# Layer 0's shift and scale by slices of 128 columns from TensorE, and the first projections accumulated slice by slice in six banks

## The chip, the cores and the metric

The kernel runs on one core of one Trainium2 chip, in float32. The metric is the device time of one execution in microseconds (us), the median over executions. TensorE is called PE, VectorE DVE, ScalarE ACT, GpSimd POOL, and the queue that issues the transfers SP. PEld is PE's weight load, which the profile lists beside its matmuls.

## The reference, cut to what matters

Two trunk layers work on 1152 tokens: 128 context tokens (tile 0) and 1024 latent tokens (tiles 1 to 8), each with 1024 channels. Every layer begins in this way:

```python
mod = (jax.nn.silu(cvec) @ w_mod + b_mod).reshape(-1, 1, 3 * D_MODEL)
shift, scale, gate = jnp.split(mod, 3, axis=-1)
h = rms_norm(x, g_pre) * (1.0 + scale) + shift
fx, fz, rq, rk, rv, rz, aq, ak, av, az, mg = split_columns(h @ w_in)
```

Context tokens use one conditioning vector (`c_ctx`), latent tokens another (`c`), so the shift and the scale are two columns of 1024 numbers each: products of two vectors with a 1024x1024 part of `w_mod` (4 MB each). From `h` come all projections of the layer; then follow Fourier mixing, retention, windowed attention, the gates and the output projection.

## The kernel before

The framework orders the instructions of each engine ahead of time by a simulated schedule in which earlier program text has the higher priority. On the chip each engine works its list in order and waits on semaphores.

**Split operands.** `h` is kept transposed (channels on partitions, tokens along the free axis) in eight slices `k` of 128 channels, as a rounded part `HH` and a remainder `HL`. A weight unit is loaded into `raw` (512 KB), rounded to `hi` by ACT and its remainder `lo` is made by POOL (`split_unit`, L174 and L175). `unit_n2` loads 256 rows by 512 columns, so one unit serves two slices `k`; four units serve one group of 512 output columns. `proj_n` (L228 to L230) multiplies a token tile by a group: for each of eight slices three matmuls of 128x128 weights by 512 columns, HH by hi, HH by lo and HL by hi, all summed in one PSUM bank.

**Banks.** PSUM has eight banks: `pj` and `sl` two each, `sc` and `pv` one each, `tr` two.

**Startup, layer 0.** `startup` does the work ahead of the first projections. `prep` of a tile takes the row norm (ACT square, DVE and POOL for the root, DVE multiply), transposes eight blocks on PE and copies them to `xT`. Three tiles are prepared. Then the scale is made: each 128x1024 row block of `w_mod` (512 KB in rows of 4 KB) is multiplied on DVE by the two conditioning columns and summed into `dacc` (L335, L337), PE transposes the sums, and DVE reduces them to `sm`. The shift is made on PE: the conditioning columns are the weights (128x2) and 512 columns of `w_mod` stream past (L360), giving two rows, which are copied (L366), transposed (L369) and added to the bias (`sh`, L370). Then HH and HL of the three tiles are written (L377, L378), and the generator `g1` of the first group (`nat_group` with columns C_RK) can run: its four weight units, then tile by tile a projection into `pj`, rotary embedding on DVE, and a store. Tiles 3 to 5 and 6 to 8 are loaded, prepared and finished (`finish`, L387 to L390) while PE projects the tiles before them.

**After the first group** come the Fourier columns (L218 to L220, 384 tokens at a time), and so on to the end of the second layer.

Of the kernel before, what the change touches and what calls it, by code (L numbers as in the profile page):

```python
# [31 lines left out]
GK = 3  # L32
# [50 lines left out]
def hybrid_step(ctx, tc, ins, cst, outs):  # L83
# [199 lines left out]
    def startup(first):  # L283
        with pool("st", side="right") as st:
            def load_x(t):
                xt = mk(st, [P, D], "x0", bufs=3)
# [3 lines left out]
            xts = [load_x(t) for t in range(3)]  # L290
            cT = mk(st, [P, KT, 2], "cT")
            SP.dma_start(cT[:, :, 0], ins["c_ctx"].rearrange("(k p) -> p k", p=P))
            SP.dma_start(cT[:, :, 1], ins["c"][0].rearrange("(k p) -> p k", p=P))
            th = mk(st, [P, KT, 2], "cth")
# [3 lines left out]
            def chunk(tag, bufs):  # L298
                return mk(st, [P, KT, CH], tag, bufs=bufs)

            def prep(t, xt, xT):

                xh = norm_x(st, xt)
                for half in range(2):
                    pt = tr([P, 4, P])
                    for kk in range(4):
                        k = half * 4 + kk
                        PE.transpose(pt[:, kk, :], xh[:, k * P : (k + 1) * P], ident)
                    ACT.copy(xT[:, half * 4 : half * 4 + 4, t % 3 * P : (t % 3 + 1) * P], pt)

            xT = chunk("xT", 1)
            for t in range(3):
                prep(t, xts[t], xT)
            macc = [pj([2, 512]) for _ in range(2)]
            dacc = [mk(st, [P, D], f"dacc{s}") for s in range(2)]
            bm = mk(st, [P, 2, KT], "bm")
            gpr = mk(st, [P, KT], "gpr")
            wms = {}

            def stage(n):  # L320
                k, c0 = n % KT, 0 if n >= KT else D
                if n % 3 == 0:
                    wms["big"] = chunk("big", 2).rearrange("p a b -> p (a b)")
                wm = wms["big"][:, n % 3 * D : n % 3 * D + D]
                last_w[0] = SP.dma_start(wm, w_mod[0, k * P : (k + 1) * P, c0 : c0 + D]).ins
                return wm

            for k in range(KT):
                wm = stage(k)
                if k == 2:  # L330
                    SP.dma_start(bm, b_mod[0, 0 : 2 * D].rearrange("(s k p) -> p s k", p=P, k=KT))
                    SP.dma_start(gpr, g_pre[0].rearrange("(k p) -> p k", p=P))
                for s in range(2):
                    if k == 0:
                        DVE.tensor_scalar(dacc[s], wm, siluc[:, k, s : s + 1], None, op0=ALU.mult)  # L335
                    else:
                        DVE.scalar_tensor_tensor(  # L337
                            out=dacc[s], in0=wm, scalar=siluc[:, k, s : s + 1], in1=dacc[s], op0=ALU.mult, op1=ALU.add
                        )
            pr = mk(st, [P, KT, 2], "dred")  # L340
            for c in range(0, KT, 2):
                pt = (sc if c % 4 else sl)([P, 2, 2, P])
                for cc in range(2):
                    for s in range(2):
                        PE.transpose(pt[:, cc, s, :], dacc[s][:, (c + cc) * P : (c + cc + 1) * P], ident)
                DVE.tensor_reduce(pr[:, c : c + 2, :], pt, axis=AX.X, op=ALU.add)
            DVE.tensor_tensor(out=sm, in0=pr, in1=bm[:, 1, :].unsqueeze(2).to_broadcast([P, KT, 2]), op=ALU.add)
# [926 lines left out]
```

## Time and profile before

| what | us |
|---|---|
| median of 3 runs | 2020.54 (2018.04 to 2021.05) |
| the profiled execution, its own time | 2026.52 |
| its span, first to last instruction | 2024.7 |
| PE busy in the span | 1968.2 |
| DVE, ACT, POOL busy | 1033.1, 676.1, 551.5 |

The profiled execution is 6 us above the median of the runs, and 1.8 us of its time lie outside the span. Busy shares are averages over stages with different limits, and matmuls overlap in the records, so that the length of one is more than the step from one to the next.

### The profile page before, as it was taken

What the parts mean: (1) busy time and instruction counts of PE and PEld (TensorE: products, weight loads), DVE (VectorE), ACT (ScalarE), POOL (GpSimd) and SP (SyncE); (2) the same over time, 40 slices, a digit from 0 to 9 for tenths busy, and PEclk for the clock granted to TensorE, in tenths of its full rate; (3) what the DMA queues carried; (4) which work ended last, traced back from release to release, by engine and by line L of the source; (5) the groups of instructions that cost most, each with busy time, mean ns of one, the idle gap of its engine ahead of it and who ended that gap; (6) DMA issues with size and microseconds to landing.
All of it is one profiled execution on the core that took longest, in us unless ns stands there. A gap on an engine that the chain in (4) does not pass through costs nothing.

```text
span 2024.7 us, 30761 instructions
## 1 busy us (share of the span) xinstructions
PE 1968.2 (97%) x11334; PEld 1818.2 (90%) x11334; DVE 1033.1 (51%) x2675; ACT 676.1 (33%) x1563; POOL 551.5 (27%) x424
## 2 busy tenths in 40 slices
PE   5999999999999999999999999999999999999998
PEld 2898888999999999999877978799999999999987
DVE  6726556545677775414674262434356655531411
ACT  3522111214444555414331212022345554531411
POOL 2222232121122221254441203122121223234342
PEclk8999999999999999999999999999999999999999
DMA  8323553434343332333344134233333333342142
GB/s 293 100 71 100 155 148 117 129 117 137 112 123 114 114 102 65 116 118 128 118 142 96 58 94 146 82 118 95 124 107 102 108 101 97 93 132 90 55 146 93
DMA packets 245190, 230.58 MB, mean 114 GB/s; under 512 B 37920, under 2 KB 215856, under 8 KB 244784
## 3 DMA queue, kind: packets, MB, share of 16 engines
q1 hardware_dynamic: 245040, 228.62, 37.5%
q8 instruction: 89, 1.46, 0.3%
q14 instruction: 61, 0.50, 0.1%
HBM read 170.14 MB, written 58.42 MB: 113 GB/s over the span
## 4 chain that ended last, share of the span: by engine, by line
PE 88%; DVE 4%; DMA 4%; issue 1%; ACT 1%; SPq 1%; POOL 0%; DVEq 0%; POOLq 0%; ACTq 0%
PE pj L218 13%; PE pj L219 13%; PE pj L220 13%; PE pj L229 5%; PE pj L228 5%; PE pj L230 5%; PE pv L1099 4%; PE tr L1092 3%; PE sl L1038 2%; PE sl L941 2%; PE sl L943 2%; PE sl L942 2%; DMA raw<-in_w_in 2%; PE pj L941 2%; PE pj L942 2%; PE sl L230 2%
## 5 line engine op out<-in xcount | busy, mean ns | idle before, releaser
L218 PE MATMUL pj<-HH,uh 128*128 128x384 f32 x1440 | 496.0, 344 | 11.9 <-DVE XL L653 5.7
L220 PE MATMUL pj<-HH,ul 128*128 128x384 f32 x1440 | 491.5, 341 | 0.0
L219 PE MATMUL pj<-HL,uh 128*128 128x384 f32 x1440 | 489.6, 340 | 0.0
L175 POOL TENSOR_TENSOR ul<-raw,uh 128x1024 fp32r<-128x1024 f32 x80 | 193.6, 2421 | 513.9 <-ACT uh L174 420.4
L218 PEld LDWEIGHTS pj<-HH,uh 128*128 128x128 f32 x1440 | 273.5, 190 | 16.7 <-DVE XL L653 6.0
L219 PEld LDWEIGHTS pj<-HL,uh 128*128 128x128 f32 x1440 | 273.7, 190 | 0.7
L220 PEld LDWEIGHTS pj<-HH,ul 128*128 128x128 f32 x1440 | 273.3, 190 | 1.0
L174 ACT CAST uh<-raw 128x1024 fp32r<-128x1024 f32 x80 | 83.9, 1049 | 176.3 <-PE pj L219 108.2
L446 DVE SCALAR_TENSOR_TENSOR macc<-mw,siluc,macc 128x256 f32<-128x256 f32 x224 | 134.1, 639 | 8.4 <-DMA mw<-in_w_mod 8.4
L228 PE MATMUL pj<-uh,HH 128*128 128x512 f32 x336 | 134.1, 400 | 3.5 <-ACT kv L546 1.9
L229 PE MATMUL pj<-ul,HH 128*128 128x512 f32 x336 | 133.5, 397 | 0.0
L230 PE MATMUL pj<-uh,HL 128*128 128x512 f32 x336 | 132.9, 396 | 0.0
L1075 ACT ACTIVATE E<-E,NM 128x640 f32<-128x640 f32 (+1 forms) x128 | 101.8, 798 | 53.0 <-DVE NM L1071 52.9
L1095 ACT CAST Eh<-tr 128x512 fp32r<-128x512 f32 (+1 forms) x136 | 76.3, 574 | 113.9 <-PE tr L1092 101.0
L1096 DVE TENSOR_TENSOR El<-tr,Eh 128x512 fp32r<-128x512 f32 (+1 forms) x136 | 90.6, 671 | 36.3 <-ACT Eh L1095 29.7
L956 POOL TENSOR_TENSOR mth<-mth,ml 128x384 f32<-128x384 f32 x48 | 52.1, 1086 | 187.6 <-DVE mth L944 144.3
L944 DVE SCALAR_TENSOR_TENSOR M<-M,sl 128x384 f32<-128x384 f32 x48 | 26.5, 553 | 133.1 <-PE sl L943 132.6
L1056 DVE CUSTOM_DVE_ANT_0 E<-sl,mask,m 128x384 f32<-128x384 f32 (+1 forms) x128 | 71.9, 580 | 30.4 <-PE sl L1038 30.0
L1092 PE MATMUL tr<-ident,E 128*128 128x128 f32 x528 | 85.6, 273 | 0.0
L228 PEld LDWEIGHTS pj<-uh,HH 128*128 128x128 f32 x336 | 63.4, 189 | 18.4 <-ACT kv L546 2.1
L1052 DVE TENSOR_SCALAR_CACHE_REDUCE E<-sc 128x256 f32<-128x256 f32 x128 | 49.3, 421 | 60.1 <-PE sc L1038 59.4
L944 DVE SCALAR_TENSOR_TENSOR mth<-mth,pj 128x384 f32<-128x384 f32 x96 | 52.9, 551 | 52.4 <-ACT mth L938 27.8
(305 smaller groups left out, 4134.8 us busy)
## 6 DMA issues: line engine op xcount, KB each, us to landing
raw<-in_w_in SPq DMA_DIRECT2D x84, 512.0 KB, 4.0
scr_m<-mth SPq DMA_DIRECT2D x96, 192.0 KB, 2.4
mw<-in_w_mod SPq DMA_DIRECT2D x128, 128.0 KB, 2.5
scr_n<-ns SPq DMA_DIRECT2D x36, 256.0 KB, 2.4
ml<-scr_m SPq DMA_DIRECT2D x48, 192.0 KB, 2.5
mrow<-scr_m SPq DMA_DIRECT2D x16, 576.0 KB, 5.1
big<-in_w_mod SPq DMA_DIRECT2D x16, 512.0 KB, 4.8
raw<-in_w_out SPq DMA_DIRECT2D x16, 512.0 KB, 4.0
```

The lines of the kernel that those rows point to most:

```text
L174: ACT.copy(hi, raw)
L175: POOL.tensor_tensor(out=lo, in0=raw, in1=f(hi), op=ALU.subtract)
L218: PE.matmul(acc, hi[:, k, :], HH[:, k, tok], start=(k == 0), stop=False)
L219: PE.matmul(acc, hi[:, k, :], HL[:, k, tok], start=False, stop=False)
L220: i = PE.matmul(acc, lo[:, k, :], HH[:, k, tok], start=False, stop=(k == KT - 1))
L228: PE.matmul(acc, a, hi[:, k % 2, :], start=(k == 0), stop=False)
L229: PE.matmul(acc, a, lo[:, k % 2, :], start=False, stop=False)
L230: i = PE.matmul(acc, b, hi[:, k % 2, :], start=False, stop=(k == KT - 1))
L446: DVE.scalar_tensor_tensor(out=accs[s], in0=w, scalar=siluc[:, k, s : s + 1], in1=accs[s], op0=ALU.mult, op1=ALU.add,)
L1075: ACT.activation(Es[hh][:, 0:nk], srcs[hh], AF.Exp, bias=NM[t][:, hs + hh : hs + hh + 1], scale=0.125, accum_out=DEN[t][:, hs + hh : hs + ...
L1092: PE.transpose(pt[:, i, hh, :], Es[hh][:, (n + i) * P : (n + i + 1) * P], ident)
L1096: DVE.tensor_tensor(out=El[:, :w], in0=pt, in1=f(Eh[:, :w]), op=ALU.subtract)
```

## The change

The startup works slice by slice instead of matrix by matrix. For each slice `k` of 128 channels it loads two 1024x128 column blocks of `w_mod` (`wm`, 512 KB each in pieces of 512 bytes, three buffers): one for the shift and one for the scale. PE multiplies them directly with the conditioning columns: the block's eight 128x128 parts are the weights and the two columns stream past, so that the result has channels on partitions and needs no transposition. DVE adds bias and gain (16 numbers become two columns of `sh` and `sm`), applies scale and shift to that slice of six prepared tiles (640 and 128 tokens), ACT writes HH, POOL writes HL, and PE adds this slice's product with the weight unit to six accumulators, one for each of tiles 0 to 5, which hold all banks except `tr`. After the eighth slice the six sums are complete. Tiles 6 to 8 follow in the old way, from loads that are queued behind the last `wm`. The bias, the gain and both conditioning vectors are loaded at the front; x tiles have four buffers, and are normalised in place; one of the two copies after a tile's transposes goes to DVE.

```diff
-    def startup(first):
+    def startup(first, us, accs, unit):
...
+            def load_wm(k):
+                w = []
+                for j in range(2):
+                    wm = mk(st, [P, KT, P], "wm", bufs=3)
+                    c0 = j * D + k * P
+                    last_w[0] = SP.dma_start(wm, w_mod[0, :, c0 : c0 + P].rearrange("(k p) f -> p k f", p=P)).ins
+                    w.append(wm)
+                return w
...
+            SP.dma_start(bm, b_mod[0, 0 : 2 * D].rearrange("(s k p) -> p s k", p=P, k=KT))
+            SP.dma_start(gpr, g_pre[0].rearrange("(k p) -> p k", p=P))
+            xts += [load_x(t) for t in range(2, 4)]
+            wms = [load_wm(0)]
...
+            for t in range(ET):
+                if t == 4:
+                    xts += [load_x(4), load_x(5)]
+                    us.append(unit(0))
+                    wms.append(load_wm(1))
                 prep(t, xts[t], xT)
...
+            for t, b in enumerate((pj, pj, sl, sl, sc, pv)):
+                accs[t] = b([P, 512])
             for k in range(KT):
+                if k + 2 < KT:
+                    if k % 2 == 0:
+                        us.append(unit(k // 2 + 1))
+                    wms.append(load_wm(k + 2))
+                pm = tr([P, 2, 2])
+                for j in range(2):
+                    for kk in range(KT):
+                        PE.matmul(
+                            pm[:, j, :], wms[k][j][:, kk, :], siluc[:, kk, :], start=(kk == 0), stop=(kk == KT - 1)
                         )
+                DVE.tensor_scalar(sh[:, k, :], pm[:, 0, :], bm[:, 0, k : k + 1], None, op0=ALU.add)
+                DVE.tensor_scalar(
+                    sm[:, k, :], pm[:, 1, :], bm[:, 1, k : k + 1], gpr[:, k : k + 1], op0=ALU.add, op1=ALU.mult
+                )
+                for s, tok in ((0, slice(0, P)), (1, slice(P, ET * P))):
+                    DVE.tensor_scalar(
+                        xT[:, k, tok], xT[:, k, tok], sm[:, k, s : s + 1], sh[:, k, s : s + 1], op0=ALU.mult, op1=ALU.add
+                    )
+                tok = slice(0, ET * P)
+                ACT.copy(HH[:, k, tok], xT[:, k, :])
+                POOL.tensor_tensor(out=HL[:, k, tok], in0=xT[:, k, :], in1=f(HH[:, k, tok]), op=ALU.subtract)
+                hi, lo = us[k // 2]
+                for t in range(ET):
+                    tk = slice(t * P, (t + 1) * P)
+                    a, b = HH[:, k, tok][:, tk], HL[:, k, tok][:, tk]
+                    PE.matmul(accs[t], a, hi[:, k % 2, :], start=(k == 0), stop=False)
+                    PE.matmul(accs[t], a, lo[:, k % 2, :], start=False, stop=False)
+                    PE.matmul(accs[t], b, hi[:, k % 2, :], start=False, stop=(k == KT - 1))
             last = last_w[0]
...
+            with tc.issue_after(last):
+                xts = [load_x(t) for t in range(ET, NT)]
+            for a, b in ((ET, 8), (8, NT)):
+                xT = mk(st, [P, KT, 2 * P], "xT2")
+                for t in range(a, b):
+                    prep(t - a, xts[t - ET], xT)
+                finish(a, b, 1, xT)
...
             for t in range(NT):
-                acc = pj([P, 8, 64])
-                proj_n(us, t, acc.rearrange("p b c -> p (b c)"))
+                if t in accs:
+                    acc = accs[t].rearrange("p (b c) -> p b c", b=8)
+                else:
+                    acc = pj([P, 8, 64])
+                    proj_n(us, t, acc.rearrange("p b c -> p (b c)"))
```

## Rows read from the trace of the kernel before

**Rows 1.** The page: busy time by engine, and the chain that ended last.
```profile
PE 1968.2 (97%) x11334; PEld 1818.2 (90%) x11334; DVE 1033.1 (51%) x2675; ACT 676.1 (33%) x1563; POOL 551.5 (27%) x424
...
PE 88%; DVE 4%; DMA 4%; issue 1%; ACT 1%; SPq 1%; POOL 0%; DVEq 0%; POOLq 0%; ACTq 0%
```

**Rows 2.** Busy time by stretch: engines, granted clock (1.00 is 2.4 GHz), DMA share, GB/s.
```profile
0.00:20.00 20.00, 5.85 (x24) 4.71 (x24) 11.09 (x16) 7.69 (x14) 2.87 (x8) 0.88 0.88 259
20.00:48.10 28.10, 20.59 (x56) 4.81 (x56) 19.21 (x35) 5.65 (x9) 7.32 (x4) 0.78 0.89 321
48.10:106.10 58.00, 57.97 (x267) 47.47 (x268) 41.90 (x115) 32.15 (x71) 16.90 (x15) 0.97 0.34 103
```

**Rows 3.** The chain in order of time, 44 to 50 us: start, length, what.
```profile
47.67 0.41 ACT HH L377
...
48.13 0.50 PE pj L228
```

**Rows 4.** The same chain later: eight transposes, and the first group's last matmul.
```profile
69.12 0.87 PE tr L308 x8
...
105.91 0.23 PE pj L230
```

**Rows 5.** Groups of PE by line and shape, 0 to 120 us.
```profile
L360 PE MATMUL pj<-big,siluc 128*2 128x512 f32 x32 | 17.9, 703 | 5.5 <-DMA big<-in_w_mod 5.5
L228 PE MATMUL pj<-uh,HH 128*128 128x512 f32 x36 | 15.0, 416 | 0.2 <-ACT HH L377 0.2
```

**Rows 6.** Timeline of the SP queue.
```profile
8.79 4.35 SPq L332 DMA_DIRECT2D gpr<-in_g_pre  x1
```

**Rows 7.** Three stretches of DMA traffic; the last two columns are share and GB/s.
```profile
12.90:15.20 2.30, 0.00 (x0) 0.00 (x0) 2.30 (x4) 0.00 (x0) 0.36 (x1) 1.00 0.83 33
15.30:23.00 7.70, 1.94 (x8) 1.57 (x8) 7.70 (x8) 1.17 (x2) 1.00 (x1) 0.50 0.99 389
...
110.00:112.00 2.00, 2.00 (x14) 2.00 (x13) 0.33 (x1) 1.40 (x2) 0.37 (x1) 1.00 0.88 259
```

**Rows 8.** Groups of the other engines by line and shape, 0 to 120 us.
```profile
L175 POOL TENSOR_TENSOR ul<-raw,uh 128x1024 fp32r<-128x1024 f32 x5 | 11.9, 2379 | 38.2 <-ACT uh L174 35.5 <-PE pj L220 2.8
...
L254 ACT ACTIVATE xh<-x 128x1024 f32<-128x1024 f32 x9 | 9.6, 1062 | 3.1 <-DMA x<-in_x_prompt 2.9 <-DMA x<-in_x_sample 0.2
...
L256 DVE TENSOR_SCALAR xh<-x,hrr 128x1024 f32<-128x1024 f32 x9 | 8.9, 985 | 2.5 <-POOL hrr L248 2.5
...
L390 POOL TENSOR_TENSOR HL<-big,HH 128x384 fp32r<-128x384 f32 x6 | 6.9, 1160 | 14.4 <-ACT HH L388 14.4
...
L309 ACT COPY big<-tr 128x512 f32<-128x512 f32 x12 | 6.6, 585 | 8.5 <-PE tr L308 8.5
...
L248 POOL TENSOR_TENSOR hrr<-hrv,mhalf 128x1 f32<-128x1 f32 x9 | 6.2, 685 | 25.3 <-DVE hrv L246 25.3
...
L353 DVE TENSOR_SCALAR xT<-xT,sm 128x256 f32<-128x256 f32 x8 | 2.7, 340 | 0.0
```

**Rows 9.** Timeline of PE in retention: small float32 products, then a projection.
```profile
276.28 1.11 PE L834 MATMUL pv<-kvq,A 128*128 128x64 f32 x8
277.19 0.48 PE L230 MATMUL pj<-xh,HL 128*128 128x512 f32 x1
```

**Rows 10.** Timeline near 45 us: four transposes of two rows.
```profile
45.15 0.41 PE L369 MATMUL tr<-ident,xh 2*128 2x2 f32 x4
```

**Rows 11.** Stretches around two falls of the granted clock (third column from the end).
```profile
45.60:47.50 1.90, 0.00 (x0) 0.00 (x0) 1.90 (x8) 0.42 (x2) 0.00 (x0) 1.00 1.07 367
...
49.30:52.50 3.20, 3.20 (x14) 2.84 (x13) 2.93 (x10) 3.20 (x10) 0.55 (x1) 0.50 0.83 234
...
1203.50:1205.40 1.90, 0.00 (x0) 0.00 (x1) 0.65 (x2) 0.27 (x1) 0.00 (x0) 1.00 0.67 176
...
1206.50:1209.70 3.20, 3.20 (x11) 2.72 (x10) 2.94 (x6) 0.27 (x1) 1.11 (x4) 0.50 0.32 107
1209.80:1212.00 2.20, 2.20 (x11) 1.75 (x10) 1.25 (x4) 0.00 (x0) 0.00 (x0) 0.99 0.40 136
```

More of the change, by code (lines that the diff above doesn't have):

```diff
@@ L340, in startup @@
[L340 to L347, printed above, removed]
@@ L348, in startup @@
-            DVE.scalar_tensor_tensor(
-                out=sm, in0=sm, scalar=1.0, in1=gpr.unsqueeze(2).to_broadcast([P, KT, 2]), op0=ALU.add, op1=ALU.mult
-            )
-            for k in range(KT):
-                for s, tok in ((0, slice(0, P)), (1, slice(P, CH))):
-                    DVE.tensor_scalar(xT[:, k, tok], xT[:, k, tok], sm[:, k, s : s + 1], None, op0=ALU.mult)
-            for k in range(KT):
-                wm = stage(KT + k)
-                if k == GK:
-                    with tc.issue_after(last_w[0]):
-                        next(first)
-                for i in range(2):
-                    PE.matmul(
-                        macc[i], siluc[:, k, :], wm[:, i * 512 : i * 512 + 512], start=(k == 0), stop=(k == KT - 1)
-                    )
@@ L363, in startup @@
-            last = last_w[0]
-            mr = mk(st, [P, D], "xh", bufs=2)
-            for i in range(2):
-                (DVE.tensor_copy if i else ACT.copy)(mr[:2, i * 512 : i * 512 + 512], macc[i])
-                pt = tr([P, 4, 2])
-                for c in range(4):
-                    PE.transpose(pt[:, c, :], mr[:2, (4 * i + c) * P : (4 * i + c + 1) * P], ident[:2, :2])
-                DVE.tensor_tensor(
-                    out=sh[:, 4 * i : 4 * i + 4, :], in0=pt,
-                    in1=bm[:, 0, 4 * i : 4 * i + 4].unsqueeze(2).to_broadcast([P, 4, 2]), op=ALU.add,
-                )
@@ L374, in startup @@
-            for s, tok in ((0, slice(0, P)), (1, slice(P, CH))):
-                for k in range(KT):
-                    b = sh[:, k, s : s + 1]
-                    ACT.activation(HH[:, k, tok], xT[:, k, tok], AF.Identity, bias=b)
-                    DVE.scalar_tensor_tensor(
-                        out=HL[:, k, tok], in0=xT[:, k, tok], scalar=b, in1=f(HH[:, k, tok]),
-                        op0=ALU.add, op1=ALU.subtract,
-                    )
+                        PE.transpose(pt[:, kk, :], xt[:, k * P : (k + 1) * P], ident)
@@ new lines, in prep @@
+                    out = xT[:, half * 4 : half * 4 + 4, n * P : (n + 1) * P]
+                    (DVE.tensor_copy if half else ACT.copy)(out, pt)
+            xT = mk(st, [P, KT, ET * P], "xT")
+            for t in range(ET):
[3 more added lines that the diff above has]
+                    wms.append(load_wm(1))
+                prep(t, xts[t], xT)
+            for t, b in enumerate((pj, pj, sl, sl, sc, pv)):
+                accs[t] = b([P, 512])
@@ L390, in finish @@
                     eng.tensor_tensor(out=HL[:, k, tok], in0=hf, in1=f(HH[:, k, tok]), op=ALU.subtract)
-            xT = chunk("big", 2)
-            for t in range(3, 6):
-                with tc.issue_after(last):
-                    xt = load_x(t)
-                prep(t, xt, xT)
-            next(first)
-            finish(3, 6, 1, xT)
-            xT = chunk("big", 2)
-            for t in range(6, NT):
-                with tc.issue_after(last):
-                    xt = load_x(t)
-                prep(t, xt, xT)
-                next(first)
-            finish(6, NT, 1, xT)
+            next(first)
+            with tc.issue_after(last):
[5 more added lines that the diff above has]
+                finish(a, b, 1, xT)
         for _ in first:
```

58 lines of the change are left out of this document (20 added, 38 removed).

## The prediction, made before the result was known

> **What bounds the kernel now.** I read the page first: PE is busy for 97% of the span and holds 88% of the chain that ended last [rows 1]. The reader is to see that a microsecond saved on another engine is worth nothing unless PE waits for it, and that a microsecond of PE work added or removed counts in full. Next I read busy time by stretch over the part that the change rewrites [rows 2]. Until 48.1 us PE does little that lasts: it is busy for 5.9 of the first 20 us and 20.6 of the next 28, and most of that is the shift's 32 instructions (17.9 us) [rows 5]. From 48.1 on PE is full. The chain shows the start: the first HH at 47.7, and the first projection at 48.13 [rows 3]. The first group's projections end at 106.1 [rows 4]. Behind that PE works without a gap on the next group, so I take one point as the measure of the change: when PE has finished the first group. It is 106.1 us now, and a shift of it moves the end by as much, less or more only by waits further on.
>
> In those 58 us lie 216 projection matmuls, six groups of 36 of which one is shown [rows 5], and 48 transposes, those of tiles 3 to 8. One projection matmul follows another at 0.233 us (the chain's pieces are 0.23 and 0.24, one is shown [rows 4]), so 216 take 50.4; 48 transposes at 0.109 (0.87 for eight [rows 4]) take 5.2; the rest is 3.2 us at half clock (1.6 lost) [rows 11] and small things.
>
> **What goes.** The DVE sums over w_mod, their transposes and reductions, the shift's 17.9 us on PE, its copies and transposes, and the separate scaling of three tiles all lie before 48.1. They vanish, and are worth exactly what the first projection comes earlier.
>
> **When the first projection can start.** It now needs six tiles prepared, not three, one weight unit and two wm blocks. Transfers: 3.5 MB of x tiles and the unit (3.67 million bytes) at the 389 GB/s that long pieces reach [rows 7] are 9.4 us. The wm blocks come in 512-byte pieces; the stretch with such pieces moved 259 GB/s at a share of 0.88, so 294 when full [rows 7], which makes 3.6 us for the first two. The four loads of 4-byte elements (20 KB) are now all ahead of x tile 2; bias and gain alone (12 KB) held the DMA for 2.3 us at 33 GB/s [rows 7] and blocked SP for 4.35 us at the gain's issue [rows 6], so all four are 3.8 us. From 2.2 us on this adds up to 19 us; the last x tile is in at about 17.5. Its prep is 1.06 + 0.2 on ACT, 0.7 for the root on POOL and a little on DVE, 0.98 on DVE, 0.6 for a copy [rows 8], and 1.94 for eight transposes at half clock (the stretch of 15.3 to 23 holds eight and nothing else on PE [rows 7]): 5.5. Then the slice's chain: DVE on 128 and 640 tokens (0.34 for 256 [rows 8], so about 1.1 together), ACT on 768 (0.59 for 512 [rows 8], so about 0.9), waits 0.3. This gives 25.3. PE itself needs until about the same time: 48 transposes at 0.24 [rows 7] from 7 us on are 11.6, the first slice's products at half clock 7. I take 26.5 for the first projection, with bounds 24 (everything overlaps) and 30 (transfers out of order). That is 21.6 us earlier than now.
>
> **What is added on PE.** The products with w_mod are 8 slices x 2 blocks x 8 parts = 128 float32 products, and a float32 product is two instructions (L834 has 4 heads x 9 tiles x 2 layers = 72 products and 144 instructions; the shift's 16 products show as 32 [rows 5]). So 256 pairs of weight load and matmul. Each streams only two columns, so the load of 128 weight columns sets the pace. No row has that shape. The nearest has the same weights and 64 columns: eight of L834 take 0.91 us, from 276.28 to the next matmul at 277.19 [rows 9], 0.114 each. The other side is the four transposes of two rows, which take 0.41 together [rows 10], with 0.2 for the length of a single one, so about 0.07 each; but a transpose is another form, with one instruction for a product. I take 0.114: 29.2 us in all. 48 of the 256 (slice 0 and half of slice 1) can run before 26.5, in idle time; 208 remain on the path: 23.7 us.
>
> The same sum from 26.5 on: projections 50.4, transposes of tiles 6 to 8 2.6, small products 0.4, w_mod products 23.7: 77.1, ending at 103.6. At 26.5 the clock is at half, as it is now at that time [rows 7]; the first projections pay 1.6 for it, as after 49.3 [rows 11]. That makes 105.2, against 106.1: a gain of 0.9 us. So the earlier start and the added weight loads cancel almost to nothing, before any stall.
>
> **Other engines, costed at nothing.** A slice on PE is 4.2 us of projection and 3.65 of products, 7.85. POOL does HL of 768 tokens (1.16 for 384 and 2.38 for 1024 [rows 8], so 1.9 to 2.3) and half a unit (1.2): 3.5 at most. ACT has 0.9 + 0.5, DVE about 1.5. A slice's transfers are 1.05 million bytes of wm and half a unit, about 4.4 us. All hide under 7.85; without cover POOL's remainder would be late first, and the third matmul of each tile would wait 1 to 2 us a slice. Three wm buffers hold a slice and a half, so PE can run at most that far ahead.
>
> **The clock, which decides.** What the rows show: PE idle from 1203.5 to 1205.4, then projections, and at 1206.5 the granted clock fell to 0.50 and stayed there for 3.2 us of dense matmuls; the same after the idle 45.6 to 47.5 (0.50 from 49.3 to 52.5) [rows 11]. So less than 2 us without matmuls has been enough for a fall to 1.2 GHz, and about 3.3 us of dense work at half speed is the price. In the changed kernel, products that stream two columns stand between projections, 3.65 us a slice, and, because projections have the earlier program text and are ready sooner, tend to run as two slices of products (7.3 us) and then two of projections (8.4 us). Whether a PE that mostly loads weights keeps its clock, no row tells: L834's eight last 0.91 us. Bounds are no fall and a fall for each of six slices. With two columns to a weight load nearly nothing streams, so I hold the stretch nearer to the idle rows than to the dense ones and take a fall for each pair after the first: three. Each costs 1.65 in dense work (3.3 us at half) and, with half of its 64 loads at half speed, 32 x 0.114 = 3.6: together 5.2, and 15.7 for three. Six falls of one slice each would be 1.65 + 16 x 0.114 = 3.5 each, 21.
>
> **The rivals.** *The clock holds* (28%). Weight loads count as work. For it: PE's queue would show no idle time at all, and both falls in the rows followed idle time. Then the sum is 105.2, or 103.6 if the front is warm too: 2018 to 2019.6, own range 2015 to 2024 with 24 and 30 for the start.
>
> *Two-column products are cheap* (7%), on the faster side. Place: the 208 pairs on the path. If they step at 0.07 as the small transposes do [rows 10], they cost 14.6 and not 23.7, and with the clock up the time is about 2010; it decides below 0.095 a pair. Against it: L834's 0.114 at 64 columns, which take half that time to stream. The Trainium skill, TensorE: Matmul & The Clock Gate, section Back-to-back issue gap, gives a floor of about 25 ns for matmuls of up to 64 columns. By that rule alone the products would cost 5.2 us and the time would be near 2001; the same section says that this leaves the weight load out, and L834's step is over four times as long, so it gets no chance beyond the 7%.
>
> *Tiles 6 to 8 come late* (7%). Their loads are queued behind the last wm, which waits until slice 6's first block has been used. With the clock up that is some 15 us before the last slice ends, and two tiles' prep and `finish` (DVE about 6 us for eight slices, then five rotary evacuations behind it) take 14 to 18. PE would wait up to 5 us, 2024 to 2026. When the clock falls, this hides.
>
> **How the numbers follow.** The forecast is that the clock falls (58%): 105.2 + 15.7 - 106.1 = 14.8 us longer. The sum is made against the profiled 2026.52, and carried over as a difference to the median of the runs, 2020.54, since the profiled execution is 6 us above it: 2035. Its own range is one fall of four microseconds to six falls and a late start: 2023 to 2044. The range must reach to the case in which the clock holds, down to 2015 (start at 24, warm), so 2015 to 2044. What 0.2% is, 4 us, is about what a measurement of this kernel tells from no change. Faster by more: 9 of the clock case's 28, the 7 of cheap products, 2 of the forecast: 18%. Within: 13 of the clock case, 3 of the forecast, 3 of the late tiles: 19%. Slower: 63%.
>
> **What would show it.** Right: first projection at 24 to 30 us; eight products' instructions stepping at 0.11 at full clock and 0.2 and more at half; granted clock 0.5 in several stretches between 35 and 110, each behind a run of products; the first group's last matmul near 121. Wrong: clock at 1.00 from 35 on (then the end near 105 and no measurable change), a step of the products well under 0.1, a first projection far from 26.5 because the list that the schedule wrote out puts PE or SP in another order than I assume, or a PE that waits between slices for HL or wm.

## The result, and the profile after

The changed kernel takes 2053.3 us (median of 4 runs, 2052.06 to 2055.11), the kernel before on the same chip 2020.8 (4 runs, 2018.04 to 2021.94). The ratio is 1.0164, with a 95% interval of 1.0146 to 1.0181: slower by 32.5 us. The forecast was slower by 14.8 us, 2035 in a range of 2015 to 2044. The direction and the clock's part in it were right; the size was not, and the time lies outside the range.

The page of the changed kernel still shows a kernel that PE bounds, as [rows 1] did; PE has 25 us more of busy time, and the products with w_mod (L347) hold 2% of the chain:

```profile
PE 1993.3 (97%) x11534; PEld 1854.7 (90%) x11534; DVE 1012.1 (49%) x2660; ACT 671.3 (33%) x1545; POOL 561.2 (27%) x432
...
PE 86%; DMA 5%; DVE 5%; issue 1%; SPq 1%; ACT 1%; POOL 1%; DVEq 0%; POOLq 0%; ACTq 0%
```

The prediction measured the change where PE has finished the first group. I take the first matmul of the Fourier columns, L218, which stands just behind it. In the timeline of PE (start, length, what) it is, in the kernel before:

```profile
107.08 0.52 PE L218 MATMUL pj<-HH,uh 128*128 128x384 f32 x1
```

and in the changed kernel:

```profile
139.37 0.34 PE L218 MATMUL pj<-HH,uh 128*128 128x384 f32 x1
```

That is 32.3 us later, and the whole time is 32.5 longer. The exact fit is partly luck: the profiled execution of the kernel before is 6 us above its median, and the two profiled spans differ by 26.7 us only (2051.4 against 2024.7), so the kernel before lost some 6 us of its profiled execution behind L218. In all runs below, the shift of this point and the shift of the time agree within 6 us.

Busy time by stretch of the changed kernel, for [rows 2] (start and end, length, then PE, PEld, DVE, ACT, POOL, the granted clock, DMA share, GB/s):

```profile
0.00:20.00 20.00, 6.92 (x32) 5.43 (x32) 6.37 (x15) 9.06 (x15) 3.31 (x10) 1.00 0.91 234
20.00:48.10 28.10, 20.30 (x86) 19.06 (x87) 6.37 (x11) 8.48 (x11) 13.81 (x8) 0.52 0.65 192
48.10:106.10 58.00, 58.00 (x293) 51.07 (x293) 10.18 (x30) 8.44 (x12) 12.58 (x9) 0.79 0.43 127
106.10:139.30 33.20, 30.37 (x144) 24.34 (x144) 26.19 (x81) 13.91 (x33) 8.25 (x9) 0.95 0.24 82
```

The clock column reads 1.00 for the first 20 us, but there it isn't to be trusted: eight transposes take 1.97 us (x8 at 9.78 in the timeline of PE), as at half clock in [rows 7]. Two things stand out. Between 20 and 48 us PE is no busier than before and runs at 0.52 of its clock. And from 48.1 to 106.1, where [rows 2] had 0.97, the granted clock is 0.79 although PE is never idle. The chain shows what stood ahead of the first projection (start, length, what; hrr is the root of a tile's row norm, L321 scales the tile, L326 transposes it, L365 is the first projection):

```profile
26.18 0.56 POOL hrr L248
...
26.77 2.84 DVE x L321
...
29.75 1.94 PE tr L326 x8
31.68 13.21 PE tr L347 x62
44.89 0.63 PE pj L365
```

The last tile's transposes end at 31.7, and behind them 62 products with w_mod run as one block of 13.2 us, 0.213 each. The first projection starts at 44.75 by the timeline, 3.4 us before that of [rows 3], where the forecast had it 21.6 earlier.

The clock, by stretch, in the same columns. The stretches from 50.80, 65.50 and 85.40 are runs of products, the others dense projections:

```profile
44.90:49.00 4.10, 4.10 (x12) 3.21 (x13) 0.00 (x0) 0.00 (x0) 0.00 (x0) 0.59 0.09 23
50.80:54.30 3.50, 3.50 (x34) 3.50 (x33) 1.27 (x4) 0.83 (x1) 1.15 (x1) 1.00 0.54 156
55.10:58.70 3.60, 3.60 (x10) 2.81 (x9) 0.69 (x2) 0.83 (x1) 1.83 (x1) 0.53 0.85 233
...
65.50:73.80 8.30, 8.30 (x56) 8.30 (x54) 1.27 (x4) 0.83 (x1) 1.81 (x1) 0.70 0.63 182
73.90:79.00 5.10, 5.10 (x13) 4.00 (x13) 1.27 (x4) 0.83 (x1) 1.83 (x1) 0.50 0.38 112
80.50:85.30 4.80, 4.80 (x25) 4.00 (x24) 0.00 (x0) 0.00 (x0) 0.00 (x0) 1.00 0.00 0
85.40:93.90 8.50, 8.50 (x58) 8.45 (x57) 1.27 (x4) 0.83 (x1) 1.81 (x1) 0.72 0.65 180
94.00:99.50 5.50, 5.50 (x13) 4.29 (x14) 1.27 (x4) 0.83 (x1) 1.83 (x1) 0.50 1.06 351
```

A run of products starts at 1.00, and in its course or just behind it the clock falls to 1.2 GHz (0.50), where it stays for 3.6 to 5.5 us of the projections that follow; then it rises, and the next run of products takes it down again. PE is busy all the time: there is no idle stretch here, as there was ahead of both falls in [rows 11].

**The balance from the first projection to L218** is 94.6 us, against 59.0 before. 216 projections at 0.233 are 50.4 in both. The 194 products behind the first projection stand in stretches of 25.7 us together, 0.109 each where the clock is up (34 of them in 3.71 us) and twice that where it is down: 21.1 at full clock and 4.5 lost to it. Dense work at half clock loses the length of its stretches times the missing share of clock: with 108.5 to 112.9 at 0.64, the five such stretches give 10.3, where the kernel before lost 1.6. PE is idle for 2.7 (0.6 at 118, 2.1 at 131.6 for the weights of the Fourier step). There are 24 transposes fewer, 2.6 us. What is left is about 3 against 1.8 before. So: -3.4 for the start, +21.1 products, +13.2 half clock (4.5 + 10.3 - 1.6), -2.6 transposes, +2.7 idle, and 1.3 not assigned: 32.3.

### The profile page after: what moved, and what is told of

Its sections match the earlier page's. It is cut to its first block, busy times and chain, and to the rows that moved or that the text cites. A ratio compares the mean times of both kernels' runs of the same rounds, so it can differ in the third digit from the quotient of the medians.

```text
span 2051.4 us, 31130 instructions
## 1 busy us (share of the span) xinstructions
PE 1993.3 (97%) x11534; PEld 1854.7 (90%) x11534; DVE 1012.1 (49%) x2660; ACT 671.3 (33%) x1545; POOL 561.2 (27%) x432
## 4 chain that ended last, share of the span: by engine, by line
PE 86%; DMA 5%; DVE 5%; issue 1%; SPq 1%; ACT 1%; POOL 1%; DVEq 0%; POOLq 0%; ACTq 0%
PE pj L218 13%; PE pj L219 13%; PE pj L220 13%; PE pj L229 4%; PE pj L228 4%; PE pj L230 4%; PE pv L1087 3%; PE tr L1080 3%; PE sl L1026 2%; PE tr L347 2%; DMA raw<-in_w_in 2%; PE sl L929 2%; PE sl L931 2%; PE sl L930 2%; PE sl L230 2%; PE sl L229 2%
## 5 line engine op out<-in xcount | busy, mean ns | idle before, releaser
L218 PE MATMUL pj<-HH,uh 128*128 128x384 f32 x1440 | 492.8, 342 | 10.5 <-ACT mth L926 3.6
L218 PEld LDWEIGHTS pj<-HH,uh 128*128 128x128 f32 x1440 | 271.4, 188 | 15.7 <-ACT mth L926 5.8
L228 PE MATMUL pj<-uh,HH 128*128 128x512 f32 x312 | 124.4, 400 | 4.3 <-ACT kv L531 2.2
L229 PE MATMUL pj<-ul,HH 128*128 128x512 f32 x312 | 123.9, 397 | 0.0
L230 PE MATMUL pj<-uh,HL 128*128 128x512 f32 x312 | 123.3, 395 | 0.0
L932 DVE SCALAR_TENSOR_TENSOR M<-M,sl 128x384 f32<-128x384 f32 x48 | 26.5, 554 | 134.9 <-PE sl L931 134.4
L932 DVE SCALAR_TENSOR_TENSOR mth<-mth,pj 128x384 f32<-128x384 f32 x96 | 52.9, 551 | 50.3 <-ACT mth L926 26.7
L228 PEld LDWEIGHTS pj<-uh,HH 128*128 128x128 f32 x312 | 59.0, 189 | 19.0 <-ACT kv L531 2.3
```

What stands on the lines that cost most here:

```text
L218: PE.matmul(acc, hi[:, k, :], HH[:, k, tok], start=(k == 0), stop=False)
L228: PE.matmul(acc, a, hi[:, k % 2, :], start=(k == 0), stop=False)
L229: PE.matmul(acc, a, lo[:, k % 2, :], start=False, stop=False)
L230: i = PE.matmul(acc, b, hi[:, k % 2, :], start=False, stop=(k == KT - 1))
```

## The experiments

All times are medians in us, and the difference and the ratio are to the kernel before on the same chip (2015.8 for e1 to e4, 2015.2 for e5 to e8, 2013.5 for e9, 2013.8 for e10). Kernels are compared by the difference column. The last two columns are starts in the one profiled execution, which need not lie at the median: it is 3.0 us above it in e4 and 3.8 below it in e5.

| kernel | time | difference | ratio, 95% interval | first projection | first L218 |
|---|---|---|---|---|---|
| before | 2020.8 | 0 | 1 | 48.13 | 107.08 |
| the change | 2053.3 | 32.5 | 1.0164 (1.0146 to 1.0181) | 44.75 | 139.37 |
| e1_wide | 2033.0 | 17.2 | 1.0076 (1.0052 to 1.0099) | 42.70 | 125.66 |
| e2_noprod | 2000.2 | -15.6 | 0.9916 (0.9897 to 0.9936) | 35.50 | 92.71 |
| e3_xfirst | 2046.3 | 30.5 | 1.0143 (1.0123 to 1.0163) | 43.32 | 136.23 |
| e4_mix | 2045.4 | 29.6 | 1.0142 (1.0116 to 1.0169) | 40.63 | 141.60 |
| e5_front | 2038.1 | 22.9 | 1.0107 (1.0089 to 1.0124) | 42.45 | 124.81 |
| e6_widemix | 2034.1 | 18.8 | 1.0093 (1.0076 to 1.0110) | 38.78 | 127.95 |
| e7_tail | 2025.3 | 10.1 | 1.0048 (1.0032 to 1.0064) | 33.74 | 119.56 |
| e8_cols | 2047.9 | 32.7 | 1.0157 (1.0139 to 1.0175) | 34.63 | 141.07 |
| e9_cols2 | 2022.4 | 8.9 | 1.0037 (1.0024 to 1.0049) | 34.92 | 111.80 |
| e10_cols3 | 2016.1 | 2.3 | 1.0007 (0.9995 to 1.0019) | 34.47 | 106.58 |

My theory was that products that stream only two columns let the clock fall. The rivals were that the products' own time or waits between slices make the loss, whatever the clock does, and that the late start of the projections does.

**e1_wide: the same products, but 128 columns stream.** The two columns are repeated 64 times by the operand's view, so the weight loads and the results stay and the stream grows. The order that the schedule wrote changes a little with it: the long runs of products are of 64 and 50 instructions, where the change has 62, 54 and 58.

```diff
-pm = tr([P, 2, 2])
+pm = tr([P, 2, 128])
...
-    pm[:, j, :], wms[k][j][:, kk, :], siluc[:, kk, :], ...
+    pm[:, j, :].rearrange("p (a b) -> p a b", b=2), wms[k][j][:, kk, :],
+    siluc[:, kk, :].unsqueeze(1).to_broadcast([P, 64, 2]), ...
...
```

> Each product with w_mod streams 128 columns (the two conditioning columns repeated 64 times) and not 2; weights, loads and result are the same, and the order that the schedule writes puts a slice's products and projections in turn. Theory A (the granted clock falls because the products stream next to nothing): granted clock at 1.00 in the product stretches from the second slice on, products stepping at 0.11 us and not 0.21, no dense matmuls at half clock behind them; 13 to 17 us faster than the changed kernel, 2036 to 2040. Theory B (the clock falls whatever the products stream, or the loss lies in waits between slices): clock as before the edit, 2050 to 2058.

Sixty-four times the columns made the kernel faster by 15.3 us: the difference is 17.2 and not 32.5, within the 13 to 17 of theory A. The granted clock is 1.00 from 40 us on. Since the order moved as well, e4 and e6 below make the same comparison with the order held. In e1 another wait shows that the change did not have. Busy time by stretch of e1:

```profile
90.00:100.00 10.00, 10.00 (x53) 8.37 (x53) 6.13 (x12) 5.25 (x9) 4.68 (x5) 1.00 0.38 149
100.00:110.00 10.00, 7.44 (x39) 5.64 (x38) 9.83 (x30) 5.28 (x15) 2.21 (x3) 1.00 0.25 92
110.00:120.00 10.00, 8.05 (x35) 6.21 (x35) 8.11 (x34) 3.49 (x12) 1.50 (x3) 1.00 0.39 123
```

PE is idle for 4.5 us between 100 and 120 while DVE is busy for 17.9 of the 20 us, with tiles 6 to 8: the rival "tiles 6 to 8 come late" of the prediction, at the place and nearly at the price (up to 5) that it gave.

**e2_noprod: the products left out.** Shift and scale are made from the conditioning columns themselves, so the products with w_mod are missing and the numbers are others. DVE, ACT and POOL have the same instructions. The transfers are the same too, but not their times: no product holds a block of w_mod back, so they run ahead (DMA share 1.13 from 20 to 35.5 us), and SP issues tile 5 behind two more blocks.

```diff
-pm = tr([P, 2, 2])
-for j in range(2):
-    for kk in range(KT):
-        PE.matmul(pm[:, j, :], wms[k][j][:, kk, :], siluc[:, kk, :], ...)
-DVE.tensor_scalar(sh[:, k, :], pm[:, 0, :], bm...)
+DVE.tensor_scalar(sh[:, k, :], siluc[:, k, :], bm...)
...
```

> The 256 product instructions are left out (shift and scale are then made from the conditioning columns, not from w_mod); all loads stay. Theory A (the products' weight loads and the clock that falls with them are the whole loss): the first projection starts about 34 and not 44.75, the first group is done near 95 and not 139, about 45 us faster than the changed kernel, 2008, and 12 faster than the kernel before. Theory B (waits between slices on DVE, ACT and POOL, or the transfers, hold PE as well): PE then waits between slices for HH or HL, and less than 30 us is gained, over 2023.

0.9916, 15.6 us faster than before, as theory A said: all the rest of the change is a gain of that size, and the products, with what hangs on them (the clock, the late release of w_mod's buffers), cost 48 us (32.5 + 15.6). The first projection, in the timeline of PE of e2 (in brackets what it waited for):

```profile
35.50 0.79 PE L359 MATMUL pj<-uh,HH 128*128 128x512 f32 x1 [2.71 <-ACT HH L353]
...
36.52 0.63 PE L359 MATMUL pj<-uh,HH 128*128 128x512 f32 x1
36.95 0.63 PE L360 MATMUL pj<-ul,HH 128*128 128x512 f32 x1
```

The first projections step at 0.43 us, half clock; from 38.9 on they step at 0.23, and the granted clock is 1.00 from 40 to 92.7. So without any product the first projection is at 35.5, nine microseconds behind the forecast's 26.5, and the change has it another 9.25 later. The two parts are rough, because e2's last transposes start 1.1 us later than the change's (30.86 against 29.75).

**e3_xfirst: x tiles ahead of the weights.** A fifth x buffer, and tile 4's load ahead of w_mod; only tile 5 stays behind the weight unit.

```diff
-xts += [load_x(t) for t in range(2, 4)]
+xts += [load_x(t) for t in range(2, 5)]
...
-    xts += [load_x(4), load_x(5)]
+    xts += [load_x(5)]
```

> Five x tiles are loaded ahead of the first wm, and the sixth ahead of the weight units (five x buffers; the square's output goes to the place that the transposes fill later, to make room). Theory A (the first projection is late because tiles 4 and 5 arrive late, at 22.5 us, and their root waits behind POOL's split): the last transposes end about 25 and not 31.7, the first projection starts about 39 and not 44.75; 5 to 6 us faster, 2047 to 2049. Theory B (the wm blocks or the products' list set the start): the same time, 2051 to 2056.

The last transposes start at 27.31 in place of 29.75, but the last 14 of the products ahead of the first projection now wait 0.8 us for w_mod, and it comes 1.4 us earlier, not the 5 to 6 of theory A. The clock falls as before. The difference is 2 us smaller than the change's, which the intervals hardly tell apart: the order of these transfers is a small part of it.

**e4_mix and e6_widemix: products spread among the projections.** Eight product instructions behind each two dense matmuls, for the next slice; ahead of the first projection only slice 0's. PE's order of instructions is the same in the two kernels through all eight slices; e4 streams two columns and e6 128.

```diff
+products(0, 0, 2 * KT)
 for k in range(KT):
...
     PE.matmul(accs[t], a, hi[:, k % 2, :], ...)
+    i = PE.matmul(accs[t], a, lo[:, k % 2, :], ...)
+    if k + 1 < KT and t < 4:
+        with tc.issue_after(i.ins):
+            products(k + 1, 4 * t, 4 * t + 4)
```

> Same work, other order on PE: only slice 0's products stand ahead of the first projection, and the products of slice k+1 stand in groups of eight instructions behind two dense matmuls each, inside slice k's projections; the HL matmuls close a slice. Theory A (long runs of products without dense work make the clock fall, and the 30 products of slice 1 ahead of the first projection delay it): first projection at 39 to 40, granted clock 1.00 from 45 on, about 12 us faster, 2039 to 2043. Theory B (any share of such products makes the clock fall): clock at 0.50 through all eight slices, 2065 and more. Theory C (order and clock don't matter, the weight loads do): 2050 to 2053.

> The run with mixed order, instruction for instruction in the same order on PE, but each product streams 128 columns instead of 2. Theory A (what the products stream decides about the clock): granted clock 1.00 from the first projection to the end of the slices, products at 0.95 us per eight throughout, 10 to 15 us faster than the mixed run with two columns. Theory B (the other order explained the gain of the first 128-column run): the same time as the mixed run within 4 us.

Busy time by stretch of e4:

```profile
50.00:60.00 10.00, 10.00 (x55) 8.85 (x55) 1.27 (x4) 0.83 (x1) 1.83 (x1) 0.80 0.31 89
...
70.00:80.00 10.00, 10.00 (x58) 8.59 (x57) 1.28 (x4) 1.36 (x2) 2.15 (x2) 0.95 0.47 138
80.00:90.00 10.00, 10.00 (x51) 8.73 (x50) 1.27 (x4) 0.83 (x1) 3.33 (x2) 0.74 0.40 116
90.00:100.00 10.00, 10.00 (x48) 8.90 (x47) 1.27 (x4) 0.83 (x1) 0.63 (x1) 0.67 0.58 172
```

and of e6:

```profile
50.00:60.00 10.00, 10.00 (x67) 8.78 (x66) 1.27 (x4) 0.83 (x1) 1.82 (x1) 1.00 0.47 138
60.00:70.00 10.00, 10.00 (x62) 8.58 (x62) 2.55 (x8) 1.04 (x2) 1.82 (x1) 1.00 0.46 132
...
80.00:90.00 10.00, 10.00 (x67) 8.73 (x65) 1.27 (x4) 1.78 (x2) 2.31 (x2) 1.00 0.76 246
90.00:100.00 10.00, 8.61 (x49) 6.99 (x48) 4.32 (x11) 3.82 (x8) 3.49 (x4) 1.00 0.04 17
...
110.00:120.00 10.00, 7.04 (x30) 5.39 (x29) 8.18 (x33) 3.87 (x13) 1.39 (x3) 0.95 0.41 127
```

This is the cleanest pair. PE is fully busy in both from 50 to 90 us; with two columns the granted clock of ten microseconds is 0.74 to 0.95, with 128 it is 1.00, and ten microseconds hold 62 to 67 matmuls and not 51 to 58. L218 comes 13.7 us earlier, the difference is 10.8 us smaller, theory A of e6. That mixing alone would hold the clock, theory A of e4, is refuted by e4, which is 29.6 and not about 20 us slower than the kernel before. Behind the slices both wait for tiles 6 to 8: PE is idle for 5.7 us between 90 and 120 in e6, and for 4.3 between 118 and 136 in e4.

**e5_front: products in the idle time of the start.** Slices 0 and 1 have their products between the transposes of the first tiles, in two banks that are free then; two columns, and e3's order of loads.

```diff
 for t in range(ET):
+    if t == 2:
+        products(0, sc)
+    if t == 5:
+        products(1, pv)
     prep(t, xts[t], xT)
```

> The changed kernel with two-column products as they were, but the products of slices 0 and 1 stand between the transposes (their results in the banks of accumulators 4 and 5, which start later), and five x tiles are loaded first. Theory A (the first projection is late because 62 product instructions at half clock stand in one block behind the last transposes, though PE is idle for half of the 22 us before): first projection at 33 to 36 and not 44.75; the clock falls later stay, so 8 to 12 us faster than the changed kernel, 20 to 24 above the kernel before. Theory B (transfers set the start): first projection at 40 or later, under 4 us gained.

This tests what the forecast had assumed, that 48 of the 256 run before the first projection at no cost. The timeline of PE in e5:

```profile
26.77 3.41 PE L338 MATMUL pv<-siluc,wm 128*128 128x2 f32 x16
...
34.20 1.95 PE L328 MATMUL tr<-ident,x 128*128 128x128 f32 x8
36.02 6.56 PE L338 MATMUL tr<-siluc,wm 128*128 128x2 f32 x30
42.45 0.77 PE L378 MATMUL pj<-uh,HH 128*128 128x512 f32 x1
```

The 64 early products do go into the start, but not for nothing: at 0.213 each (half clock) they take 13.6 us, the last transposes start at 34.20 where e3, with the same loads, has them at 27.31, and 30 products of slice 2 stand ahead of the first projection. It gains 2.3 us only and misses the 33 to 36 of theory A. The group's end gains 14.6 and the time 9.6, of which e3's order of loads has 2: 94 products and not 62 are done before projections begin, and the clock is 1.00 from 50 to 60, where the change has a stretch at 0.53. How the gain divides between the two was not tried. Behind 60 us the clock falls as in the change (0.66 in 60 to 70, 0.50 in 90 to 100).

**e7_tail: the parts that helped, together.** e5's start, e6's mixing with 128 columns, and tiles 6 to 8 loaded from slice 2 on; tiles 6 and 7 are prepared in slice 3 and scaled in slices 4 to 7.

```diff
+if k == 2:
+    late = [load_x(t) for t in range(ET, NT)]
...
+if k == 3:
...
+    for t in (6, 7):
+        prep(t - 6, late[t - 6], xT2)
+if k >= 4:
+    for kk in (2 * k - 8, 2 * k - 7):
+        finish_k(kk, 6, 8, xT2)
```

> 128-column products, mixed order, products of slices 0 and 1 between the transposes, and tiles 6 to 8 loaded during the slices, prepared there, and tiles 6 and 7 finished slice by slice from slice 4 on. Theory A (what is left against the kernel before is the products' weight loads on PE, 192 after the first projection at 0.11, and a few us of waits): first projection near 31, first group done near 110, 2 to 6 us above the kernel before. Theory B (waits for tiles 6 to 8 were no loss): 10 to 15 above, as the 128-column run without it.

1.0048, the clock 1.00 from 40 to 110. At 10.1 us above the kernel before it is 8.7 better than e6, but not at theory A's 2 to 6; L218 is at 119.56, where A had 110. The first projection is at 33.74, 14.4 us earlier than in the kernel before. Behind it, 192 products at 0.11 are 21 us and PE's waits 6.9, of which 3.5 ahead of a late tile's projections: more than the start gains.

**e8_cols, e9_cols2 and e10_cols3: the roles exchanged.** The conditioning columns, padded to 32, become the weights and 128 columns of w_mod stream; the eight row blocks go in two rounds of four, each block of a round to its own group of 32 columns of the array, at partitions 0, 32, 64 and 96 of one bank. All else is e7's. A small product with a matrix of ones and zeros (`sel`) adds the four groups and turns the rows into columns.

```diff
-    pm[:, j, :], wms[k][j][:, kk, :], siluc[:, kk, :], ...
+    pms[k][32 * g : 32 * g + 32, j, :], silp[:, 4 * h + g, :], wms[k][j][:, 4 * h + g, :], ...
...
+ACT.copy(cp, pms[k])
+for j in range(2):
+    PE.matmul(pm[:, j, :], cp[:, j, :], sel, start=True, stop=True)
```

> As the run before it, but the conditioning columns are the weights (32 columns wide, 30 of them zero), w_mod streams past, and four parts go to four column groups of the array (results on partitions 0, 32, 64 and 96), summed and transposed by two small products a slice. Theory A (weight loads of 128 columns are the price; groups of columns work side by side): a slice's 32 instructions take about 0.9 us and not 3.6, first group done near 97, 8 to 12 us faster than the kernel before. Theory B (the groups run one behind the other): 3.4 us a slice and the two small products on top, 5 to 10 us slower than the kernel before.

The timeline of PE in e8, around one slice:

```profile
41.82 0.42 PE L346 MATMUL tr<-wm,silp 128*32 128x128 f32 x8
42.17 0.50 PE L405 MATMUL pj<-uh,HH 128*128 128x512 f32 x1
...
47.64 0.50 PE L356 MATMUL tr<-sel,pmc 128*128 128x2 f32 x4
50.41 0.79 PE L405 MATMUL pj<-xh,HH 128*128 128x512 f32 x1 [2.27 <-ACT HH L399]
```

Eight product instructions step to the next matmul in 0.35 us, 0.044 each, against 0.109 in the change. But the sum (L356) stands behind all projections of the slice in PE's list, so copy, sum, DVE and ACT are waited for at each slice: seven waits of 16.5 us together, and the clock goes down with them (0.66 to 0.87 by ten microseconds from 50 to 120). The price of the products came near theory A's (32 in 1.4 us, where it had 0.9), but the kernel is 32.7 us slower than the kernel before, not 8 to 12 faster: 1.0157.

e9 only moves this chain: slice k+2's products stand in slice k, and slice k+1's sum behind the first tile of slice k.

```diff
+if k + 1 < KT and t == 0:
+    chain(k + 1, i.ins)
+if k + 2 < KT and t == 4:
+    with tc.issue_after(i.ins):
+        products(k + 2, tr, 0, 2 * KT)
+    copy(k + 2)
```

> As e8_cols, with the same products by column groups (weights: 32 padded columns of the conditioning vectors, 128 columns of w_mod stream), but the chain behind them is taken off the path: slice k+2's products run in slice k, behind its fifth tile; slice k+1's sum over the groups runs behind slice k's first tile, so that copy, sum, DVE, ACT and POOL have most of a slice of projections before them. Theory A (e8 lost its time to PE waiting for that chain and to the clock that fell in these waits; the products themselves are 0.05 us an instruction): first projection at 33 to 35 us, granted clock 1.00 from about 45 to 100, a slice of 4.2 us of projections and 0.8 to 1.3 of products, PE idle under 0.5 us ahead of a slice's first HH matmul; the first group's end at 98 to 108 (33 + 50.4 + 2.6 + 10 for products, and gaps for tiles 6 to 8), ratio to before 0.995 to 1.003. Rival B (transfers of w_mod in 512-byte pieces set the pace of a slice once the products are short, 1.05 MB and half a unit in 4.4 us or more against a slice of 5.2): PE waits for wm ahead of products in the middle slices, 1 us or more a slice, end at 110 to 118, ratio 1.003 to 1.007. Rival C (short column-group products still let the clock fall without any wait): 0.50 to 0.85 behind each batch of products, end at 115 to 130.

1.0037 and L218 at 111.80, both in the ranges of rival B, but not for its reason. Behind the first projection w_mod is waited for twice ahead of products (0.6 and 1.2 us), rival B in a small form. The clock is 1.00 from 40 to 70, so rival C falls. Two long waits remain, in the timeline of PE in e9:

```profile
28.41 1.08 PE L346 MATMUL pv<-wm,silp 128*32 128x128 f32 x16 [6.09 <-DMA wm<-in_w_mod]
...
73.60 0.80 PE L412 MATMUL pj<-uh,HH 128*128 128x512 f32 x1 [3.59 <-ACT HH L371]
```

The first is slice 1's products, with tile 5's transposes queued behind them. The second comes from DVE, which has tiles 6 and 7 to scale ahead of slice 5's chain in its list, and 6.0 us at half clock follow it (0.50 from 73.6 to 79.6). e10 puts both in another order, and with that loads and prepares tiles 6 and 7 one slice later.

```diff
-if t == 5:
-    products(1, pv, 0, 2 * KT)
...
+with tc.issue_after(ends[1]):        # behind tile 5's transposes and the first sum
+    products(1, pv, 0, 2 * KT)
...
+with tc.issue_after(ends[0]):        # behind the last slice's chain on DVE
+    for kk in range(KT):
+        finish_k(kk, 6, 8, xT2)
```

> As e9_cols2, with its two longest waits of PE taken away by order alone: slice 1's products, which waited 6.1 us for their w_mod blocks ahead of tile 5's transposes, now stand behind those transposes and the first sum; and DVE's scaling of tiles 6 and 7, which stood ahead of slice 5's chain (PE idle 3.6 us and then six microseconds at half clock), now stands behind the last slice's chain. Theory A (what e9 still loses is these two waits and the half clock behind them): first projection at 31 to 33 us, no wait over 1.5 us between 40 and 90, first L218 at 101 to 107 against 111.8, ratio to before 0.998 to 1.002. Rival B (the waits move: tiles 6 and 7 are now late at the end of the slices, or w_mod's transfers, which had their own waits of 0.6 and 1.2 us, take over): as much as 4 us of PE idle just ahead of tile 6's projections or ahead of products, first L218 at 108 to 113, ratio 1.002 to 1.004.

1.0007 (0.9995 to 1.0019), as fast as the kernel before and 30 us faster than the change: theory A's ratio and its range for L218 (106.58, against 107.08 before), but not its first projection, nor its "no wait over 1.5 us". In the timeline of PE in e10 these are the longest waits from the first projection on, with L218:

```profile
34.47 0.79 PE L412 MATMUL pj<-uh,HH 128*128 128x512 f32 x1 [1.63 <-ACT HH L371]
74.67 0.50 PE L412 MATMUL pj<-xh,HH 128*128 128x512 f32 x1 [1.28 <-ACT HH L371]
86.08 0.50 PE L228 MATMUL pj<-uh,HH 128*128 128x512 f32 x1 [2.31 <-ACT ns L568]
...
106.58 0.34 PE L218 MATMUL pj<-HH,uh 128*128 128x384 f32 x1
```

The first projection, expected at 31 to 33, has hardly moved (34.92 to 34.47): tile 5's transposes now start at 27.46, not 29.42, but the first sum, DVE and ACT behind them take until then. The gain is between 40 and 80, where PE is idle for 1.3 us in all and the clock is 1.00. The last wait stands ahead of tile 6's projections, where rival B had one, but what it waits for is a bank that ACT must copy out, 2.3 us, with 3.4 us at half clock behind it (0.50 from 87.0 to 90.4).

No version beats both kernels. The Trainium skill, TensorEngine Tiling (Array Packing), section When to Use Tiling, names this exchange of weights and stream for a moving side of up to 64 columns, with four column groups at 32. The trace of e8 agrees that a product's instruction is cheaper so (0.044 against 0.109), and e8 to e10 show that here it pays only when the chain behind it is off PE's path.

## Why the prediction was wrong, point by point

**The step that failed is the first projection at 26.5 us**, "21.6 us earlier than now". It came at 44.75, 3.4 us earlier than in the kernel before, and this alone is 18.2 us, more than the whole miss of 17.5 (32.3 where 14.8 was forecast). It failed in two halves of about equal size. The forecast has tile 5 prepared at 23.0 (17.5 + 5.5) and the first projection 3.5 later. In the changed kernel the last copy of tile 5 ends at 32.4, and the first projection is 12.3 later.

*9.4 us: tile 5 is prepared late.* The forecast had the last x tile in at 17.5 by adding up bytes. But SP issues tiles 4 and 5 only at 15.30, behind two weight units and a third block of w_mod. SP's queue in the changed kernel, for [rows 6]:

```profile
9.80 3.21 SPq L203 DMA_DIRECT2D raw<-in_w_in  x1
13.06 0.47 SPq L299 DMA_DIRECT2D wm<-in_w_mod  x1
13.57 1.61 SPq L203 DMA_DIRECT2D raw<-in_w_in  x1
15.30 0.86 SPq L287 DMA_DIRECT2D x<-in_x_sample  x2
```

With a second unit and a third block, the forecast's own rates give 22.1 in place of 19 (an estimate: 4.19 million bytes at 389 GB/s, 1.57 at 294, 3.8 and 2.2 us), and all of them stand ahead of the last x tile. ACT has to wait for tile 4 until 22.57. That is 5 of the 9.4. Then the row norm's root stands behind POOL's split of a weight unit (22.33 to 24.63), and DVE's scaling of tile 5, costed at 0.98, takes 2.83 beside the next split. The timeline of ACT, DVE and POOL in the changed kernel:

```profile
22.57 1.06 ACT L319 ACTIVATE x<-x 128x1024 f32<-128x1024 f32 x1 [0.32 <-DMA x<-in_x_sample]
...
25.22 0.75 DVE L321 TENSOR_SCALAR x<-x,hrr 128x1024 f32<-128x1024 f32 x1 [1.31 <-POOL hrr L248]
...
26.70 2.35 POOL L175 TENSOR_TENSOR ul<-raw,uh 128x1024 fp32r<-128x1024 f32 x1
26.77 2.83 DVE L321 TENSOR_SCALAR x<-x,hrr 128x1024 f32<-128x1024 f32 x1 [0.73 <-POOL hrr L248]
...
31.72 0.69 DVE L328 COPY xT<-tr 128x512 f32<-128x512 f32 x1 [1.52 <-PE tr L326]
```

The prediction put POOL's splits into the steady slices, where they hide, and not into the start. e3 shows that the order of two loads is not all of it (1.4 us), and in e10 the DMA is full until 30 us and the start stays at 34.47: which of transfers, POOL and DVE would be the last to go was not tried one by one.

*Another 8.8: "48 of the 256 can run before 26.5, in idle time".* None did. PE works its list in order, and the list had all 48 transposes of six tiles ahead of any product, so PE stood idle for 6.9 us ahead of tile 4's at 26.1, although slice 0's blocks had been issued at 8.7 and a block's median time to landing was 6.1 (e5 runs their products from 16.58); and then 62 products, slice 1's with slice 0's, ran ahead of the first projection at 0.213. The words "can run" took an idle engine for a free one. e5 puts the products into the start and is 7.6 us better than e3, which has the same loads, though its first projection comes only 0.9 earlier: they delay the transposes there.

**The products at 0.114** were right: 0.109 at full clock and 0.213 at half. L834 at 64 columns was the right row to go by. 194 and not 208 lay behind the first projection, 21.1 us at full clock where 23.7 was forecast. The cheap-products rival falls. By the 25 ns floor that the prediction quoted from the Trainium skill, TensorE: Matmul & The Clock Gate, section Back-to-back issue gap, they would have taken under a quarter of what the trace shows.

**The clock** was the right mechanism. There were four falls and not three, each in or behind a long run of products. They lost 13.1 us where 15.7 was put for them, and the start at half clock lost 1.7 where 1.6 was put. That the total came so near is partly luck: 8.6 of it is in dense work and 4.5 in products, where the forecast had 5.0 and 10.8. e4 against e6 shows that it is the two-column stream, not waits or order, that takes the clock down.

**The other engines at nothing** held within the slices: HL takes 1.82 on POOL and is never waited for from 45 to 118 us. Tiles 6 to 8 were hidden in the change but for 0.6 us, as was said for the case in which the clock falls; in e1 and e6, where it holds, PE waits 4.5 and 5.7 us for them. But in e3, e4 and e5, where it falls, PE waits 3.6 to 4.3 us at the same place, so that the clock decides this is not shown. PE's idle 2.1 us at 131.6, for weights of the Fourier step, was a term that the forecast did not have.

**The first group's end as the measure** of the change held: it moved by 32.3, the time by 32.5, with the reservation made above.

## What to carry to other kernels

Where work is moved into an idle stretch of an engine, read in that engine's own list what stands ahead of it: an engine that waits in order is idle, but not free. Here a product of 128 weight columns and a two-column stream cost 0.109 us an instruction and took the clock from the matmuls around it. Where the shapes are like these, try to let the wide side stream and make the narrow one the weights, packed side by side, and then look for who waits for the result. And before a big term of a sum is taken over, cost the start with every split, root and load that the new order puts ahead of the last tile.

## What the runs showed of the hardware that was not expected

- PE's clock can fall while PE has no idle time at all: 0.50 from 73.9 to 79.0, behind 54 products that loaded weights without a gap and streamed two columns each. With the same loads and 128 columns it was 1.00 from 40 us to the end of the slices (e1, e6). In e4 the two-column products stood in eights between dense matmuls, and the clock still fell.
- A DVE operation on 128x1024 float32 that takes 0.75 us took 2.83 when POOL's subtraction had begun 0.07 us earlier, and ended 0.55 after it (29.60 against 29.05). The Trainium skill, SBUF — State Buffer, section Who interferes with whom, says that some DVE instructions, `tensor_scalar` among them, can need the pair of ports that DVE shares with GpSimd, and that the one issued first holds it for its whole length. The trace agrees: POOL was first, and DVE's operation ended only after it.
- Float32 products with 32 columns of weights, in four groups at partitions 0, 32, 64 and 96, run at 0.044 us an instruction at full clock, with 128 columns streaming.
